# Second layer's queries and output gates of a Hawk/HGRN2 trunk: one Silu activation in place of a tanh and a VectorE product

## The chip, the cores and the metric

The kernel runs on one core of a Trainium2 chip. The time is the device time of one launch in microseconds, the median of several runs. The profiled execution is a further launch; its span runs from the first to the last instruction that the profiler records.

## What is computed

One inference step of a trunk of two layers with a model width of 1024, on 1024 prompt positions and on 8 sequences of 4 sample positions. Layer one is an RG-LRU block (convolution, gates, a linear recurrence, an output gate with SiLU). Layer two is an HGRN2 layer with eight heads of 128 keys and 128 values. The change lies in layer two, of which the reference says:

```python
def _hgrn_layer(x, g_norm, w_in, lb, o_gain, w_out, S0):
    xn = _rmsnorm(x, g_norm)
    u = (xn @ w_in).astype(jnp.float32)
    q, f, iv, gate = jnp.split(u, 4, axis=-1)
    q = jax.nn.silu(q).reshape(Bsz, T, H_B, DK_B)
...
    o, S_T = _hgrn2_chunked(q, k, v, log_g, S0)
    o = o * lax.rsqrt(jnp.mean(o * o, axis=-1, keepdims=True) + EPS) * o_gain.reshape(H_B, DV_B).astype(jnp.float32)
    y = (o.reshape(Bsz, T, INNER_B) * jax.nn.silu(gate)).astype(x.dtype)
    return x + y @ w_out, S_T.astype(x.dtype)
```

So silu(z) = z * sigmoid(z) is taken of the queries `q` and of the output gate `gate`. The forget gate `f` goes through a sigmoid. The keys, the decay and the values need no silu. The attention output `o` is linear in `q` and is normalized per head, so a constant factor on `q` cancels in the norm if the norm's epsilon is scaled with it.

## The kernel before

All activations lie transposed, features on the 128 partitions and the 1056 positions (1024 + 32) along the columns. Every product of weights and activations is made of three single-pass products of float32 values split into a high and a low part (`mm3`, L241 to L245: high times high, high times low, low times high), so TensorE does three matmuls for each product, and ScalarE, VectorE and GpSimd make the parts: ScalarE casts the high part (L380, L461, L1373, L1430), VectorE or GpSimd subtracts to get the low one (L325).

The order of the work is not written out by hand. Each operation is given to a planner, `Flow` (L52 to L199), with its engine, an estimated duration, the keys that it reads and writes, and a priority; the planner lays out a schedule and then emits the instructions of each engine in that order. Every engine runs its own instructions in order. There are two such plans. The first (L300 to L926) holds layer one and the first products of layer two; after it has found a schedule it also makes 3000 random trials (`search`, L167, with `SEARCH` at L24) that reshuffle operations of the first 60 estimated microseconds. These trials draw from the list of operations, so another list of operations gives another draw. The second plan (L929 to L1744) holds the rest, without random trials. Operations of TensorE marked `main` keep the order in which they are given.

Layer one ends with `out_last` (L650): for each of three column chunks of 352 it adds the output projection to the residual, sums squares for the norm (L432, L435), and scales and splits the normalized activations (`scaled_parts`, L458). L529 and L531 are evacuations of layer one's gates in its first chunk. Then come the first products of layer two, `first1` (L708): the queries of the first head (`i == 0`, L716 and L717) and its forget gate (`i == 1`, L720 to L722).

Layer two works head by head. For the first two heads, `item` (L996) evacuates each product of 352 columns: it takes the tanh of half the product on ScalarE (L1009) into a buffer `t`, one of a ring of five, and then, for the forget gate (`i == 1`), makes the decay row and the key row on GpSimd (L1012, L1014), and for the queries (`i == 0`) and the output gate (`i == 3`) computes (tanh(z/2) + 1) * z on VectorE (L1018). Since silu(z) is half of that, the row holds 2 silu(z). The values (`i == 2`) are only copied (L1004). Meanwhile `build` (L1349) makes sums and differences of activation blocks on VectorE (L1370), with casts on ScalarE and residues `t` on GpSimd. With them the six heads from the third on make each pair of projections with seven block products instead of eight (`seven`, L1403): results are added up on VectorE (`plus`, L1502) and each finished quarter of 264 columns goes to `settle` (L1505), which for queries and output gates takes the tanh (L1517) into the row itself and multiplies in place on VectorE (L1518).

What a head does besides its projections hangs in four `burst`s (L1332 to L1346), placed between the products of the projections: `own_gate` (L1063) scales the query row by the decay on VectorE (L1066), `levels01` to `levels3264` make the masked attention by levels of doubling block length (small matmuls at L1054, L1108, L1139, between rescalings of the rows by `scale`, L1036 to L1045), `states`, `advance` and `outs` carry the recurrent state, and `gated` (L1310) multiplies the normalized output by half the output gain, `hog`, and by the gate row (L1327). Two constants absorb the factor 2 of the rows: `hog` (L796), and `4 * EPS` in the norm (L1299).

A change of the function that ScalarE evaluates may need its table exchanged; the compiled program then holds a load of the table (ACT_TABLE_LOAD in the profile) ahead of the activation.

Of the kernel before, what the change touches and what calls it, by code (L numbers as in the profile page):

```python
# [19 lines left out]
ALU = mybir.AluOpType  # L20
# [191 lines left out]
def tile_trunk(ctx: ExitStack, tc: tile.TileContext, xT, prm, hc, w0, wg, wo0, w1, wo1, s_in,  # L212
# [22 lines left out]
    def pv(name):  # L235
        return P[:, PRM[name][0]:PRM[name][1]]
# [26 lines left out]
    def small(n):  # L263
        a = sm[:, smn[0]:smn[0] + n]
        smn[0] += n
        return a
# [31 lines left out]
    with ExitStack() as l0:  # L298
# [409 lines left out]
        def first1(i, c):  # L708

            if i not in ws1:  # L710
                ws1[i] = weights(w1[i], 1024)
            ps, pk = product(ws1[i], xcols(c), 1)
            q = chunk(c)
            if i == 0:
                o, ok = pairs[1][:, 0, q], [("R", 1, 0, c)]
                act(CH, lambda: S.activation(o, ps[:, :CH], AF.Tanh, scale=0.5), (pk,), ok, 0)  # L716
                dve(CH, lambda: V.scalar_tensor_tensor(o, o, 1.0, ps[:, :CH], op0=ALU.add, op1=ALU.mult), (pk, *ok), ok, 0)  # L717
            else:
                t, tk = next(ts)
                act(CH, lambda: S.activation(t, ps[:, :CH], AF.Tanh, scale=0.5), (pk,), (tk,), 0)  # L720
                for o, a, b, ks in ((ST, lc, lbc, [("ST", j, c) for j in range(3)]), (a_rows[0], lcn, lc, [("a", 0, c)])):
                    pool(CH, lambda o=o, a=a, b=b: G.tensor_scalar(o[:, q], t, a[:, :1], b[:, :1], op0=ALU.mult, op1=ALU.add),  # L722
                         (tk, ("sm1",)), ks, 0)
# [49 lines left out]
        def smalls1():  # L773
            def v(f, *a, **k):
                seq((("sm1",),), 6, ("DVE", lambda: f(*a, **k)))

            def ttv(o, a, b, op):
                v(V.tensor_tensor, o, a, b, op=op)

            nonlocal lc, lcn, lbc, hog  # L780
            mx, e0, e1, lb, lc, lcn, lbc, hog = (small(8) for _ in range(8))
            ttv(mx, pv("l0"), pv("l1"), ALU.max)
            ttv(e0, pv("l0"), mx, ALU.subtract)
            ttv(e1, pv("l1"), mx, ALU.subtract)
            seq((("sm1",),), 6, ("ACT", lambda: S.activation(e0, e0, AF.Exp)))
            seq((("sm1",),), 6, ("ACT", lambda: S.activation(e1, e1, AF.Exp)))
            ttv(mx, e0, e1, ALU.add)
            v(V.reciprocal, mx, mx)
            ttv(e0, e0, mx, ALU.mult)
            ttv(e1, e1, mx, ALU.mult)  # L790
            ttv(e1, e0, e1, ALU.add)
            ttv(lb, e1, e0, ALU.subtract)
            v(V.tensor_scalar, lc, lb, -0.5, 0.5, op0=ALU.mult, op1=ALU.add)
            v(V.tensor_scalar, lcn, lc, -1.0, None, op0=ALU.mult)
            ttv(lbc, lb, lc, ALU.add)
            v(V.tensor_scalar, hog, pv("og"), 0.5, None, op0=ALU.mult)  # L796

        def masks():

# [35 lines left out]
            v(V.tensor_scalar, bt, bf, 3.0, None, op0=ALU.is_le)  # L835
            ttv(bm, bm, bt, ALU.mult)

        hbr = hbi = hbd = cn = cp = lc = lcn = lbc = hog = None
# [90 lines left out]
    with ExitStack() as l1:  # L929
# [44 lines left out]
        def brow(h, i):  # L974
            return (Bs, eight("B")) if i else (B2, eight("B2"))
# [20 lines left out]
        def item(h, i):  # L996


            def evac(c, ps, pk):
                q = chunk(c)  # L1000
                ps = ps[:, :CH]
                if i == 2:
                    n = min(CH, SEQ - c * CH)
                    act(n, lambda: S.copy(VT[:, c * CH:c * CH + n], ps[:, :n]), (pk,), (("VT", c),), 0)  # L1004
                    if n < CH:
                        thrice(vrep, ps[:, n:], (pk,), "vrep")
                    return
                t, tk = next(ts)
                act(CH, lambda: S.activation(t, ps, AF.Tanh, scale=0.5), (pk,), (tk,), 0)  # L1009
                if i == 1:  # L1010
                    g, (b, bk) = Gs, brow(h, 1)
                    pool(CH, lambda: G.tensor_scalar(g[:, q], t, lc[:, h:h + 1], lbc[:, h:h + 1], op0=ALU.mult, op1=ALU.add),  # L1012
                         (tk,), GK, 0)
                    pool(CH, lambda: G.tensor_scalar(b[:, q], t, lcn[:, h:h + 1], lc[:, h:h + 1], op0=ALU.mult, op1=ALU.add),  # L1014
                         (tk,), bk, 0)
                else:
                    o, k = (SG[h], ykeys(h % 2, c * CH, CH)) if i else arow(h, 0)
                    dve(CH, lambda: V.scalar_tensor_tensor(o[:, q], t, 1.0, ps, op0=ALU.add, op1=ALU.mult), (pk, tk), k, 0)  # L1018

            return w1[4 * h + i], evac  # L1020

# [241 lines left out]
        def outs(h, s, sk):  # L1263
# [23 lines left out]
            for i in range(3):  # L1287
# [7 lines left out]
                else:  # L1295
                    pk = sk
                    act(128, lambda: S.activation(ons, o, AF.Square, accum_out=ssq[:32, 8:9]), (pk,), (("on", 2), ("ssq", 2)), 2)
                    r = slice(8, 9)
                dve(4, lambda r=r: V.tensor_scalar(rst[:, r], ssq[:, r], 1.0 / 128, 4 * EPS, op0=ALU.mult, op1=ALU.add),  # L1299
                    (("ssq", i),), (("rst", i),), 2)  # L1300
                fl.add("POOL", 0.85, lambda r=r: G.tensor_tensor(rst[:, r], rst[:, r], mhalf[:, r], op=ALU.pow),
                       (("rst", i),), (("rst", i),), 2)
# [7 lines left out]
        def gated(h, s, sk):  # L1310
            got = []
            for i in range(2):
                ps, pk = next(hg)

                def emit(i=i, ps=ps):
                    for n in range(4):
                        T.transpose(ps[:, n * 128:(n + 1) * 128], on[:, 4 * i + n, :], ident)

                pe(0.45, emit, (("kt", i),), (pk,))
                got.append((ps, pk, i * 512, 512))  # L1320
            o = s[:, 256:288]
            pe(0.17, lambda: T.transpose(o, ons, ident[:32, :32]), (("on", 2),), (sk,))
            got.append((o, sk, 1024, 32))
            yield
            for ps, pk, a, n in got:
                w = SG[h][:, a:a + n]
                dve(n, lambda ps=ps, w=w: V.scalar_tensor_tensor(w, ps, hog[:, h:h + 1], w, op0=ALU.mult, op1=ALU.mult),  # L1327
                    (pk,), ykeys(h % 2, a, n), 3)
            if h < H - 2:
                dma(yd[h], SG[h], ykeys(h % 2, 0, TOK), (("yd", h),), 4, 528)  # L1330
# [72 lines left out]
        def seven(h, a, b, order, at=()):  # L1403
# [4 lines left out]
            def ending(i, *args):  # L1408

                free = {0: 1, 1: 2}.get(i, 0)  # L1410
                postponed.append((free, lambda: settle(h, i, *args, args[2][0] == "s")))
                flush()

            def flush():
# [90 lines left out]
        def settle(h, i, a, c, ck, own):  # L1505

            q = slice(a, a + QT)
            if i == 1:
# [5 lines left out]
            else:  # L1514
                o, k = (SG[h], ykeys(h % 2, a, QT)) if i else arow(h, 0)
                k = k if i else k[a // QT::4]
                act(QT, lambda: S.activation(o[:, q], c, AF.Tanh, scale=0.5), (ck,), k, 0)  # L1517
                dve(QT, lambda: V.scalar_tensor_tensor(o[:, q], o[:, q], 1.0, c, op0=ALU.add, op1=ALU.mult), (ck, *k), k, 0, own)  # L1518


        dma(si.rearrange("p b v -> p (b v)"), s_in[0], (), two("si"), 4, 512)
# [293 lines left out]
```

## Time and profile before

| | |
|---|---|
| median of 3 runs | 1060.99 us (1060.94 to 1062.35) |
| span of the profiled execution | 1059.4 us |
| TensorE busy | 1050.1 us, 99% |
| VectorE busy | 842.2 us, 79% |
| ScalarE busy | 590.9 us, 56% |
| GpSimd busy | 540.0 us, 51% |
| table loads on ScalarE | 26, of 1283 ns each |

The median of the runs is 1.6 us above the span of the profiled execution. Lines such as L1018 are line numbers of the kernel before. In the profile PE is TensorE, DVE VectorE, ACT ScalarE, POOL GpSimd, and SP the engine that issues most transfers. Layer one's products fill the time up to about 500 us, the first two heads of layer two lie between about 490 and 595 us, the six others end at about 950 us, and the output projection and the last norm follow.

### The profile page before, as it was taken

How to read it: one execution, taken by the hardware profiler on the slowest of the kernel's cores; microseconds unless marked ns; L12 is line 12 of the kernel's file. 1: busy time of each engine (PE TensorE's matmuls, PEld its weight loads, DVE VectorE, ACT ScalarE, POOL GpSimd, SP SyncE). 2: the span in 40 equal slices, each digit the busy share in tenths (PEclk: the TensorE clock that was granted, in tenths of full speed). 3: DMA queues.
4: the chain of work that ended last, by engine and by line, in shares of the span. 5: the costliest groups of instructions: out<-in, count | busy, mean ns of one | idle time of the engine just before them, and what ended most of it. 6: DMA issues, size and time to landing. Idle time of an engine off the chain costs nothing.

```text
span 1059.4 us, 25677 instructions
## 1 busy us (share of the span) xinstructions
PE 1050.1 (99%) x9964; PEld 1021.2 (96%) x9964; DVE 842.2 (79%) x1671; ACT 590.9 (56%) x1339; POOL 540.0 (51%) x601
## 2 busy tenths in 40 slices
PE   9999999999999999999999999999999999999997
PEld 9999999999999999999999999999999999999986
DVE  7999996888888689265799988988979797994536
ACT  6568656877775875233354474646464555652324
POOL 3425343444544366555667555555545565551544
PEclk9999999999999999999999999999999999999998
DMA  8201112123842595340211121212121221355204
GB/s 297 68 27 45 54 51 74 57 60 100 255 145 63 177 294 162 127 136 28 71 44 38 45 101 44 92 45 92 35 91 54 72 70 66 117 177 167 84 3 164
DMA packets 70121, 103.07 MB, mean 97 GB/s; under 512 B 9200, under 2 KB 50160, under 8 KB 70000
## 3 DMA queue, kind: packets, MB, share of 16 engines
q1 hardware_dynamic: 67696, 98.67, 29.2%
q10 hardware_dynamic: 2304, 2.77, 0.8%
q8 instruction: 78, 1.28, 0.5%
q14 instruction: 43, 0.35, 0.1%
HBM read 71.05 MB, written 25.49 MB: 91 GB/s over the span
## 4 chain that ended last, share of the span: by engine, by line
PE 89%; DVE 6%; DMA 2%; POOL 1%; issue 1%; ACT 0%; ACTq 0%; POOLq 0%; DVEq 0%; SPq 0%
PE mm L243 24%; PE mm L244 24%; PE mm L245 24%; PE hg L569 1%; PE hg L1054 1%; PE hg L1163 1%; DVE R L1370 1%; PE hg L1273 1%; DMA wraw<-in_w_dram 1%; PE hg L1219 1%; PE hg L243 1%; PE hg L244 1%; PE hg L245 1%; PE hg L1275 1%; DVE tmp L1370 1%
## 5 line engine op out<-in xcount | busy, mean ns | idle before, releaser
L243 PE MATMUL mm<-xh,whi 128*128 128x352 f32 (+1 forms) x1143 | 358.6, 314 | 0.0
L245 PE MATMUL mm<-xh,wlo 128*128 128x352 f32 (+1 forms) x1143 | 353.2, 309 | 0.0
L244 PE MATMUL mm<-xl,whi 128*128 128x352 f32 (+1 forms) x1143 | 353.1, 309 | 0.0
L325 POOL TENSOR_TENSOR wlo<-wraw,whi 128x256 fp32r<-128x256 f32 (+3 forms) x184 | 203.3, 1122 | 178.6 <-ACT whi L380 81.2
L244 PEld LDWEIGHTS mm<-xl,whi 128*128 128x128 f32 x1143 | 215.1, 188 | 1.5
L243 PEld LDWEIGHTS mm<-xh,whi 128*128 128x128 f32 x1143 | 214.7, 188 | 1.5
L245 PEld LDWEIGHTS mm<-xh,wlo 128*128 128x128 f32 x1143 | 214.8, 188 | 0.0
L501 DVE SCALAR_TENSOR_TENSOR k<-xb,prm_sb,k 128x352 f32<-128x352 f32 (+2 forms) x144 | 90.1, 637 | 10.9 <-ACT k L498 7.7
L243 PE MATMUL mm<-t,whi 128*128 128x264 f32 (+1 forms) x306 | 89.3, 292 | 0.0
L244 PE MATMUL mm<-t,whi 128*128 128x264 f32 (+1 forms) x306 | 87.7, 287 | 0.0
L245 PE MATMUL mm<-t,wlo 128*128 128x264 f32 (+1 forms) x306 | 87.4, 286 | 0.0
L1503 DVE TENSOR_TENSOR k<-mm,k 128x264 f32<-128x264 f32 x144 | 60.2, 426 | 20.5 <-PE mm L245 17.4
L325 POOL TENSOR_TENSOR wlo<-R,whi 128x256 fp32r<-128x256 f32 x64 | 60.1, 959 | 24.7 <-ACT whi L1430 24.7
L584 POOL TENSOR_TENSOR k<-X 128x352 f32<-128x352 f32 x36 | 44.9, 1257 | 47.8 <-DVE R L585 38.6
L380 ACT CAST whi<-wraw 128x512 fp32r<-128x512 f32 (+2 forms) x83 | 46.1, 574 | 30.1 <-PE mm L244 16.1
L243 PEld LDWEIGHTS mm<-t,whi 128*128 128x128 f32 x306 | 57.6, 188 | 0.2
L245 PEld LDWEIGHTS mm<-t,wlo 128*128 128x128 f32 x306 | 57.7, 188 | 0.0
L244 PEld LDWEIGHTS mm<-t,whi 128*128 128x128 f32 x306 | 57.6, 188 | 0.0
L1430 ACT CAST whi<-wraw 128x512 fp32r<-128x512 f32 x52 | 32.1, 618 | 36.3 <-PE mm L245 16.8
L243 PE MATMUL mm<-yh,whi 128*128 128x352 f32 x153 | 49.9, 326 | 0.0
L245 PE MATMUL mm<-yh,wlo 128*128 128x352 f32 x153 | 49.4, 323 | 0.0
L244 PE MATMUL mm<-yl,whi 128*128 128x352 f32 x153 | 49.4, 323 | 0.0
(481 smaller groups left out, 2634.3 us busy)
## 6 DMA issues: line engine op xcount, KB each, us to landing
wraw<-in_w_dram SPq DMA_DIRECT2D x90, 256.0 KB, 2.7
wraw<-in_wo_dram SPq DMA_DIRECT2D x34, 192.0 KB, 2.5
si<-in_s_in_dram SPq DMA_DIRECT2D x8, 512.0 KB, 3.8
out_ss_out_dram<-si SPq DMA_DIRECT2D x8, 512.0 KB, 2.6
R<-in_w_dram SPq DMA_DIRECT2D x15, 256.0 KB, 2.5
sg<-x1b SPq DMA_DIRECT2D x21, 176.0 KB, 2.9
x<-sg SPq DMA_DIRECT2D x21, 176.0 KB, 1.8
R<-td SPq DMA_DIRECT2D x72, 44.0 KB, 2.0
```

What stands on the lines that cost most here:

```text
L243: T.matmul(out, wh, xh, start=first, stop=False)
L244: T.matmul(out, wh, xl, start=False, stop=False)
L245: T.matmul(out, wl, xh, start=False, stop=last)
L325: emit = lambda: e.tensor_tensor(b, x, a.bitcast(F32), op=ALU.subtract)
L380: act(m, lambda hi=hi, raw=raw, m=m: S.copy(hi[:, :m], raw[:, :m]), rk, (hk,), prio)
L501: dve(u, lambda src=src, dst=dst, sh=sh, k=k: V.scalar_tensor_tensor(dst, sh(src, k), pc("cw", 12 * k + m), dst, op0=ALU.mult, op1=ALU.add ...
L569: fl.add("PE", 0.62, lambda ps=ps, i=i, c=c: T.matmul(ps[:96, :CH], gs[:, i, :], ST[:96, chunk(c)], start=True, stop=True), (("gs",), *((" ...
L584: pool(CH, lambda x=x, a=a, b=b: G.tensor_tensor(x, a.bitcast(F32), b.bitcast(F32), op=ALU.add), (ak, bk), (xk,), 3)
L1054: T.matmul(ps[32 * j:32 * j + 32, n * w:n * w + w], B[:, o:o + 32], q(slice(o, o + 32)), start=True, stop=True, tile_position=(0, 32 * j))
L1370: dve(n, lambda: V.tensor_tensor(o, a, b, op=op), r, (w,), prio, True)
L1430: act(512, lambda: S.copy(hi, raw), (rk,), (hk,), 2)
L1503: dve(QT, lambda: V.tensor_tensor(o[0], z[0], u[0], op=ALU.add), (z[1], u[1]), (o[1],), 0)
```

## The change

Queries and output gates of layer two are made by one Silu activation on ScalarE, straight from the product (first two heads: from PSUM into the row; the others: from the quarter's sum into the row). The VectorE products of L717, L1018 and L1518 are gone, and the ring of `t` buffers is used by the forget gate alone. The rows now hold silu(z) instead of twice that, so the norm's epsilon is `EPS` instead of `4 * EPS`, and the gain is used as it is instead of halved; the small array `hog` and the instruction that makes it are gone. The forget gate keeps its tanh. No transfer is added or removed. Since the list of operations differs in both plans, both are planned anew.

```diff
@@ first1
             if i == 0:
                 o, ok = pairs[1][:, 0, q], [("R", 1, 0, c)]
-                act(CH, lambda: S.activation(o, ps[:, :CH], AF.Tanh, scale=0.5), (pk,), ok, 0)
-                dve(CH, lambda: V.scalar_tensor_tensor(o, o, 1.0, ps[:, :CH], op0=ALU.add, op1=ALU.mult), (pk, *ok), ok, 0)
+                act(CH, lambda: S.activation(o, ps[:, :CH], AF.Silu), (pk,), ok, 0)
@@ smalls1
-            mx, e0, e1, lb, lc, lcn, lbc, hog = (small(8) for _ in range(8))
+            mx, e0, e1, lb, lc, lcn, lbc = (small(8) for _ in range(7))
...
-            v(V.tensor_scalar, hog, pv("og"), 0.5, None, op0=ALU.mult)
@@ item, evac
-                t, tk = next(ts)
-                act(CH, lambda: S.activation(t, ps, AF.Tanh, scale=0.5), (pk,), (tk,), 0)
                 if i == 1:
+                    t, tk = next(ts)
+                    act(CH, lambda: S.activation(t, ps, AF.Tanh, scale=0.5), (pk,), (tk,), 0)
...
                 else:
                     o, k = (SG[h], ykeys(h % 2, c * CH, CH)) if i else arow(h, 0)
-                    dve(CH, lambda: V.scalar_tensor_tensor(o[:, q], t, 1.0, ps, op0=ALU.add, op1=ALU.mult), (pk, tk), k, 0)
+                    act(CH, lambda: S.activation(o[:, q], ps, AF.Silu), (pk,), k, 0)
@@ outs
-                dve(4, lambda r=r: V.tensor_scalar(rst[:, r], ssq[:, r], 1.0 / 128, 4 * EPS, op0=ALU.mult, op1=ALU.add),
+                dve(4, lambda r=r: V.tensor_scalar(rst[:, r], ssq[:, r], 1.0 / 128, EPS, op0=ALU.mult, op1=ALU.add),
@@ gated
-                dve(n, lambda ps=ps, w=w: V.scalar_tensor_tensor(w, ps, hog[:, h:h + 1], w, op0=ALU.mult, op1=ALU.mult),
+                dve(n, lambda ps=ps, w=w: V.scalar_tensor_tensor(w, ps, pc("og", h), w, op0=ALU.mult, op1=ALU.mult),
@@ settle
-                act(QT, lambda: S.activation(o[:, q], c, AF.Tanh, scale=0.5), (ck,), k, 0)
-                dve(QT, lambda: V.scalar_tensor_tensor(o[:, q], o[:, q], 1.0, c, op0=ALU.add, op1=ALU.mult), (ck, *k), k, 0, own)
+                act(QT, lambda: S.activation(o[:, q], c, AF.Silu), (ck,), k, 0)
```

More of the change, by code (lines that the diff above doesn't have):

```diff
@@ L778, in ttv @@
                 v(V.tensor_tensor, o, a, b, op=op)
-            nonlocal lc, lcn, lbc, hog
-            mx, e0, e1, lb, lc, lcn, lbc, hog = (small(8) for _ in range(8))
+            nonlocal lc, lcn, lbc
+            mx, e0, e1, lb, lc, lcn, lbc = (small(8) for _ in range(7))
             ttv(mx, pv("l0"), pv("l1"), ALU.max)
@@ L836, in masks @@
             ttv(bm, bm, bt, ALU.mult)
-        hbr = hbi = hbd = cn = cp = lc = lcn = lbc = hog = None
+        hbr = hbi = hbd = cn = cp = lc = lcn = lbc = None
         items = gate(0) + conv(0, True)
@@ L1410, in ending @@
                 free = {0: 1, 1: 2}.get(i, 0)
-                postponed.append((free, lambda: settle(h, i, *args, args[2][0] == "s")))
+                postponed.append((free, lambda: settle(h, i, *args)))
                 flush()
@@ L1503, in plus, with settle @@
             dve(QT, lambda: V.tensor_tensor(o[0], z[0], u[0], op=ALU.add), (z[1], u[1]), (o[1],), 0)
-        def settle(h, i, a, c, ck, own):
+        def settle(h, i, a, c, ck):
             q = slice(a, a + QT)
```

## The prediction

> **What bounds the kernel now.** I read the page's busy shares first, then the granted clock, then what TensorE waited for over the whole run, then busy time head by head, then the time lines at the places where TensorE did wait.
>
> ```profile
> span 1059.4 us, 25677 instructions
> PE 1050.1 (99%) x9964; PEld 1021.2 (96%) x9964; DVE 842.2 (79%) x1671; ACT 590.9 (56%) x1339; POOL 540.0 (51%) x601
> core 0: 1059.4 us, clock 0.996
> ```
>
> TensorE (PE) is busy 99% of the span at a granted clock of 0.996, so no clock is to be won. VectorE (DVE), from which the change takes work, is busy 79%. The most that its relief can give is what TensorE now loses by waiting for it. The whole-run list of TensorE's waits has five rows (us in total, times, longest):
>
> ```profile
> PE hg L730 <- DVE ones L255: 1.0, 1, 1.0
> PE hg L1108 <- DVE a L1036: 0.5, 1, 0.5
> PE mm L243 <- DVE sg L529: 0.5, 1, 0.5
> PE mm L1683 <- DVE sg L1673: 0.4, 1, 0.4
> PE hg L1054 <- DVE R L1066: 0.4, 1, 0.4
> ```
>
> Together 2.8 us of 1059.4. Only L1108 and L1054 lie at the second layer's beginning, where VectorE loses work; L730 and L529 belong to the start, L1683 to the last norm. Most of the removed instructions belong to the six heads from the third on (L1403 to L1518). Two windows of one head's length, two lengths apart:
>
> ```profile
> 688.40:745.10 56.70, 56.70 (x820) 54.82 (x813) 47.58 (x105) 30.66 (x80) 31.64 (x37) 1.00 0.20 68
> 801.80:858.50 56.70, 56.70 (x820) 54.82 (x813) 47.58 (x105) 30.66 (x80) 31.64 (x37) 1.00 0.20 69
> ```
>
> The columns are window, length, then busy us and count of PE, weight loads, DVE, ACT, POOL. TensorE is busy for the full 56.70 us with the same 820 instructions each time; VectorE has 9.1 us idle in each (56.70 - 47.6), ScalarE (ACT) 26. The heads repeat to the hundredth of a microsecond and none of the five waits lies in them: they are TensorE's alone.
>
> **The change part by part.** VectorE loses the products of L717, L1018 and L1518, and one operation of 8 columns at L796:
>
> ```profile
> L717 DVE SCALAR_TENSOR_TENSOR R<-R,mm x3: 521/521/522, 490.0 to 506.8; 128x352 f32<-128x352 f32 x3
> L1018 DVE SCALAR_TENSOR_TENSOR sg<-k,mm x6: 505/510/522, 517.2 to 592.6; 128x352 f32<-128x352 f32 x6
> L1018 DVE SCALAR_TENSOR_TENSOR R<-k,mm x3: 506/507/521, 542.0 to 551.6; 128x352 f32<-128x352 f32 x3
> L1518 DVE SCALAR_TENSOR_TENSOR sg<-sg,k 128x264 f32<-128x264 f32 x24 | 13.8, 595 | 0.0
> L1518 DVE SCALAR_TENSOR_TENSOR R<-R,k 128x264 f32<-128x264 f32 x24 | 13.4, 562 | 0.2 <-ACT R L1517 0.2
> ```
>
> That is 3 x 0.521 + 9 x 0.51 + 13.8 + 13.4 = 33.4 us of VectorE.
>
> *Heads three to eight: 0.* The 27.2 us of L1518 are 4.5 us a head; TensorE's full windows hide them, and VectorE's idle time only grows from 9.1 to about 13.6 us. The built program has TensorE's instructions in layer two in the same order as before, so nothing moves there.
>
> *L717: 0.* The step behind it waited for GpSimd (POOL), not for it:
>
> ```profile
> 506.82 0.52 DVE L717 SCALAR_TENSOR_TENSOR R<-R,mm 128x352 f32<-128x352 f32 x1 [3.20 <-ACT R L716]
> 511.09 1.27 DVE L1066 TENSOR_TENSOR R<-R,ST 128x1056 f32<-128x1056 f32 x1 [3.74 <-POOL ST L722]
> ```
>
> From 511.09 on VectorE has hardly a gap, so three L1018 at 517, 521 and 524 us push back what follows. The chain of work gives them 0.43 us each from start to start, and TensorE waits at 540:
>
> ```profile
> 517.28 0.43 DVE sg L1018
> 521.15 0.43 DVE sg L1018
> 524.46 0.43 DVE sg L1018
> ...
> 534.66 0.75 PE L1054 MATMUL hg<-R,sg 128*32 128x32 f32 x64
> 535.35 0.43 PE L243 MATMUL mm<-xh,whi 128*128 128x352 f32 x1
> ...
> 539.37 0.76 PE L1054 MATMUL hg<-R,sg 128*32 128x32 f32 x64
> 540.63 0.69 PE L1108 MATMUL hg<-R,a 128*16 128x16 f32 x64 [0.50 <-DVE a L1036]
> ```
>
> *First wait: -0.57.* The undisturbed group of 64 takes 535.35 - 534.66 = 0.69 us to the next instruction, the waiting one 540.63 - 539.37 = 1.26; the loss is 0.57. Without the three products VectorE reaches `a` of L1036 3 x 0.43 = 1.3 us sooner. In the order of the built program the same 30 sums of L1370 stand ahead of it as before, so that 1.3 us arrives whole. 1.3 is more than 0.57.
>
> *Second wait: -0.6, between 0 and -0.7.* The second head's start at 566 waits for L1066 and then for GpSimd's L1014 (0.3 us, in the view of L1054's waits):
>
> ```profile
> 562.46 0.47 ACT L1009 ACTIVATE k<-mm 128x352 f32<-128x352 f32 x1
> 563.57 0.97 DVE L1370 TENSOR_TENSOR tmp<-xh,tmp 128x264 f32<-128x264 f32 x1 [1.12 <-POOL t L325]
> 564.23 0.82 POOL L1012 TENSOR_SCALAR ST<-k,smalls 128x352 f32<-128x352 f32 x1
> 565.03 2.43 POOL L1014 TENSOR_SCALAR a<-k,smalls 128x352 f32<-128x352 f32 x1
> 565.25 1.24 DVE L1066 TENSOR_TENSOR R<-R,ST 128x1056 f32<-128x1056 f32 x1
> 566.55 1.44 PE L1054 MATMUL hg<-R,a 128*32 128x64 f32 x62 [0.36 <-DVE R L1066]
>   POOL a L1014: 0.3, 1
> ```
>
> The tanh is done at 562.93, but GpSimd takes it up at 564.23, behind residues (`t`, L325) whose inputs VectorE made late. Six L1018 less by then are 2.6 us; the built program puts one such residue in place of three between GpSimd's last two pairs but one, and two more L1370 (some 0.9 us) ahead of L1066. GpSimd can then start as much as 1.3 us sooner, and both waits, 0.4 + 0.3, mostly go. If GpSimd is late anyway, nothing goes. I take 0.6, near the rows.
>
> *ScalarE: 0, between 0 and +1.3.* Each tanh becomes one Silu on the same engine, 60 in all, with the same shapes. No Silu is in the trace; the nearest rows are the tanh itself and a plain copy:
>
> ```profile
> L1009 ACT ACTIVATE k<-mm 128x352 f32<-128x352 f32 x12 | 5.5, 461 | 4.4 <-PE mm L245 4.4
> L1004 ACT COPY sg<-mm 128x352 f32<-128x352 f32 (+1 forms) x6 | 2.6, 440 | 0.2 <-PE mm L245 0.2
> 83.01 1.28 ACT L588 ACT_TABLE_LOAD   x1
> 84.30 1.09 ACT L588 ACTIVATE R<-R 128x1056 f32<-128x1056 f32 x1
> 489.48 0.46 ACT L716 ACTIVATE R<-mm 128x352 f32<-128x352 f32 x1 [2.76 <-PE mm L245]
> ```
>
> 440 and 461 ns differ by 5%, so Silu gets tanh's duration. The built program has one table load more than before, 27 for 26, ahead of the first L716, and none between Silu and tanh after it. The load takes 1.28 us and its successor starts 0.01 us later; before L716 ScalarE was idle for 2.76 us, which hides it. Without that cover the eviction of one bank and what queues behind it (the next L716, then casts L461) would be 1.3 us late.
>
> *First layer: 0, between -1.0 and +3.* No removed operation but L796 runs there early, but the schedule is planned anew, and the first sixth of TensorE's order and much of VectorE's come out differently. VectorE is the tight engine there, and TensorE just waits for it as it enters the second third of the columns (next start 0.45 later instead of 0.16):
>
> ```profile
> 25.00:50.00 25.00, 24.42 (x152) 23.32 (x151) 24.41 (x55) 14.98 (x33) 9.77 (x11) 1.00 0.29 91
> 42.35 0.32 PE L243 MATMUL mm<-xh,X 128*128 128x352 f32 x1
> 42.80 0.44 PE L244 MATMUL mm<-xl,X 128*128 128x352 f32 x1
> L435 DVE TENSOR_TENSOR R<-R,xo x14: 509/522/1433, 20.4 to 46.8; 128x352 f32<-128x352 f32 x14
> ```
>
> In the new order two more sums of L435 and one product of L531 less stand ahead of that point: about one half-microsecond instruction late. Elsewhere a wait may go: L529's 0.5 and the 0.29 here are there to be lost. I take 0.
>
> Sum: -0.57 - 0.6 = -1.2 us. The profiled execution would go from a span of 1059.4 to 1058.2. The median of the runs, 1060.99, lies 1.6 us over that span; with the same 1.6 the forecast is **1059.8 us**. About 0.2%, 2.1 us, is what a measurement of this kernel can tell from no change: faster means below 1058.9, slower above 1063.1.
>
> **The rivals.**
>
> *Given back.* The wait at 540 goes, but GpSimd's L1014 (2.43 us while L1066 runs beside it, at 565) keeps the second, and the start loses half a microsecond: -0.57 + 0.5 = 0, **1060.9**. For it: GpSimd, not VectorE, ends the wait of 1.12 us at 563.57. Against: its inputs come from VectorE.
>
> *More waits go.* Besides the two, the new order loses L529's 0.5 us and the 0.29 at 42.8: -1.3 - 0.8 = -2.1, **1058.7**, and a little more if smaller stalls beside them go too. Against: nothing in the change aims there.
>
> *Slower, by the start.* In the first 60 us VectorE works without a gap (24.41 of 25 us), in order. Each instruction that the new order puts ahead of the second third's residues makes TensorE 0.43 to 0.5 us late once the slack is used up, and at 42.35 there is none. It turns the sign with the third such instruction (3 x 0.45 = 1.35 against -1.2) and is measurably slower with the eighth: +3.6 - 1.2 = +2.4, **1063.4**, and upwards. For it: VectorE's order there is changed in dozens of places. Against: I count about one.
>
> *Tables switched at each turn.* Were Silu's table without tanh, the order of the built program would switch 21 times, 21 x 1.28 = 27 us of ScalarE; its 26 us idle in each head hide most, a late eviction may cost 1 to 2 us: **1062**. Against: one load more in the program, and the trace of before has no more loads than the 26 of its program. The Trainium skill has the rule behind this rival: in "ScalarE activation tables: per-element evaluation and per-set limits", section "What a function is on this engine", functions of one set need no switch, and functions of two sets are one load of 1283 ns apart, which the 1.28 us above agrees with. The Trainium skill's page "ScalarE: Activation LUTs", section "What ACT_TABLE_LOAD costs", makes a switch about 2.66 us with a drain, so 21 of them an estimated 56 us by that page; the rows at 83.01 and 84.30 leave no room for a drain, and the measured 1.28 decides.
>
> *The change does what it sounds like.* 33.4 us less of VectorE end the run 33.4 us sooner: **1027.6**. Against: 99% and five waits.
>
> **How the numbers follow.** Forecast 0.44; given back 0.21; more waits go 0.19; slower by the start 0.13; tables 0.02; all of VectorE's time 0.01. Of these, "more waits go" lies about the bound and counts as faster: 0.19 + 0.01 = 0.20. Forecast, given back and tables are within 0.2%: 0.67, slightly less for tables: 0.66. Slower: 0.14. The range takes in all but the tails of both start cases and the last: 1057.4 (both waits, the start's -1.0 and a little more) to 1063.2 (no gain at 566, +3 at the start). The likeliest alone: 1058.9 to 1060.4.
>
> **What would show it.** Right: no tanh-then-product pair left; the windows of the heads still 56.70 us with VectorE near 43; the L1108 wait gone from TensorE's list and L1054's smaller; 27 table loads of 1.28 us; Silu near 461 ns for 352 columns. Wrong: heads shorter than 56.70 (then VectorE did hold TensorE there); a new wait of TensorE before 60 us; table loads after 510 us other than the last norm's; L1108 still waiting.

## The result, and the profile after

| | before | after |
|---|---|---|
| median of the runs, on one chip | 1061.13 us (1060.94 to 1062.35) | 1069.91 us (1069.4 to 1071.14) |
| span of the profiled execution | 1059.4 us | 1067.3 us |
| VectorE busy | 842.2 us | 816.2 us |
| table loads on ScalarE | 26 | 27 |

The changed kernel is slower: the ratio is 1.0084, with a 95% interval of 1.007 to 1.0098. The forecast was 1059.8 us, and 1069.9 us lies outside its range, on the other side of no change. Lines of the changed kernel are one to three lower than those of before (L1036 is L1034, L1054 is L1052, L1108 is L1106, L1370 is L1368, L1503 of some experiments is L1501).

The head of the page after, the line on its clock, and the five longest of the seven rows of what TensorE waited for (us in total, times, longest):

```profile
span 1067.3 us, 25614 instructions
PE 1054.5 (99%) x9964; PEld 1026.1 (96%) x9964; DVE 816.2 (76%) x1610; ACT 589.2 (55%) x1340; POOL 526.4 (49%) x601
core 0: 1067.3 us, clock 0.996
```

```profile
PE hg L1052 <- DVE sg L1034: 2.9, 1, 2.9
PE hg L729 <- DVE nr L442: 1.0, 1, 1.0
PE mm L1680 <- DVE sg L1670: 0.8, 1, 0.8
PE hg L1106 <- DVE a L1034: 0.5, 1, 0.5
PE mm L243 <- DVE k L1501: 0.5, 1, 0.5
```

VectorE's busy time fell by 26.0 us; the removed instructions had 33.4, so those that stay take 7.4 us longer. TensorE is still busy 99% of the span, with the same 9964 matmuls in 4.4 us more. So part of the loss is a new wait, 2.9 us at L1052, and part is not a wait at all: matmuls that are slower.

To see where, take the n-th matmul of one trace beside the n-th of the other; beyond the start both kernels issue them in the same order. The difference of their starts (after minus before) changes in five stretches. (The spans differ by 7.9 us; the profiled execution of after, 1069.42 us, is one of its two shortest.)

| stretch of before | difference at its end | gained or lost in it |
|---|---|---|
| start, to 63 us | +0.8 | -0.8 |
| layer one, to 518 us | +3.3 | -2.5 |
| beginning of layer two, to 561 us | +7.6 | -4.2 |
| second head's start, to 581 us | +7.0 | +0.5 |
| other heads, to 966 us | +8.2 | -1.2 |

**Layer one** is not late by waits. The same window of both kernels (busy us and count of PE, weight loads, DVE, ACT, POOL), first of before, then of after:

```profile
125.00:150.00 25.00, 25.00 (x159) 25.00 (x159) 23.54 (x45) 16.16 (x33) 10.55 (x15) 1.00 0.17 52
```

```profile
125.00:150.00 25.00, 25.00 (x157) 25.00 (x157) 24.06 (x51) 17.24 (x35) 11.59 (x15) 1.00 0.17 52
```

TensorE is full in both, at a granted clock of 1.00 in both, and gets through 157 matmuls where it got through 159. The mean distance between the starts of neighbouring 352-column matmuls is 159.3 ns before and 161.3 ns after in this window; in other windows the difference is as large or smaller, and over the 455 us it adds up to the 2.5 us above, with nothing to be seen in the list of waits.

**The beginning of layer two** holds the new wait. VectorE and GpSimd in the time line of after (start, length, engine, line, out<-in), just ahead of it:

```profile
514.31 1.27 DVE L1064 TENSOR_TENSOR R<-R,ST 128x1056 f32<-128x1056 f32 x1 [7.58 <-POOL ST L721]
...
538.88 0.42 DVE L1368 TENSOR_TENSOR R<-R,xh 128x264 f32<-128x264 f32 x1
539.34 2.85 DVE L1368 TENSOR_TENSOR R<-R,xl 128x264 f32<-128x264 f32 x2
...
543.91 1.22 DVE L1034 TENSOR_TENSOR R<-R,sg 128x512 f32<-128x512 f32 x1
545.05 0.68 DVE L1034 TENSOR_TENSOR sg<-sg 128x512 f32<-128x512 f32 x1
```

```profile
538.93 2.97 POOL L325 TENSOR_TENSOR wlo<-wraw,whi 128x512 fp32r<-128x512 f32 x2 [0.26 <-PE hg L1052]
541.86 2.73 POOL L325 TENSOR_TENSOR t<-R,t 128x264 fp32r<-128x264 f32 x3
```

The forecast rested on the 30 sums that stand between own_gate and the scalings of L1036. Their busy time in that stretch, first before (L1370, to 540.50), then after (L1368, to 546.95):

```profile
511.09:540.50 29.41, 14.61 (x30) 1.00 0.17 53
```

```profile
514.30:546.95 32.65, 18.71 (x30) 0.99 0.19 64
```

They are the same 30, and take 4.1 us longer. Half of that is in two sums of L1368: 0.42 us each when alone, they take 2.85 us together while two residues run on GpSimd beside them. The rest is spread over other sums, and L1034 at 543.91 adds another 0.5 us. In the kernel before those two residues ran only at 541.77, and at that place GpSimd was the one that waited, 3.99 us for two residues `t`, while VectorE went through L1036 at 0.67 us apiece:

```profile
537.83 3.99 POOL L325 TENSOR_TENSOR t<-R,t 128x264 fp32r<-128x264 f32 x2 [1.97 <-ACT t L1373]
541.77 3.19 POOL L325 TENSOR_TENSOR wlo<-wraw,whi 128x512 fp32r<-128x512 f32 x2
```

```profile
538.01 0.68 DVE L1036 TENSOR_TENSOR R<-R,sg 128x512 f32<-128x512 f32 x1
538.61 0.67 DVE L1036 TENSOR_TENSOR sg<-sg 128x512 f32<-128x512 f32 x1
```

TensorE pays in after, in its time line and in the windows (the column behind the five engines is the granted clock):

```profile
545.79 0.76 PE L1052 MATMUL hg<-R,sg 128*32 128x32 f32 x64 [2.88 <-DVE sg L1034]
547.09 0.73 PE L1106 MATMUL hg<-R,a 128*16 128x16 f32 x64 [0.53 <-DVE a L1034]
...
573.75 1.10 PE L1052 MATMUL hg<-R,a 128*32 128x64 f32 x64
```

```profile
543.00:546.60 3.60, 0.76 (x64) 0.65 (x64) 3.60 (x6) 1.85 (x4) 1.58 (x2) 0.99 0.19 68
546.60:550.00 3.40, 2.92 (x72) 2.91 (x73) 3.37 (x8) 1.39 (x3) 0.00 (x0) 0.50 0.02 5
```

Behind the wait the granted clock is halved for 3.4 us, and the matmuls of that stretch cost another 1.1 us. The last of the three rows above has no wait: the second head's start, which waited for L1066 in before, no longer does.

### The profile page after: what moved, and what is told of

It is laid out like the page before. It is cut to its first block, busy times and chain, and to the rows that moved or that the text cites. A ratio compares the mean times of both kernels' runs of the same rounds, so it can differ in the third digit from the quotient of the medians.

```text
span 1067.3 us, 25614 instructions
## 1 busy us (share of the span) xinstructions
PE 1054.5 (99%) x9964; PEld 1026.1 (96%) x9964; DVE 816.2 (76%) x1610; ACT 589.2 (55%) x1340; POOL 526.4 (49%) x601
## 4 chain that ended last, share of the span: by engine, by line
PE 90%; DVE 6%; issue 1%; DMA 1%; POOL 1%; ACT 0%; ACTq 0%; POOLq 0%; DVEq 0%
PE mm L243 25%; PE mm L244 24%; PE mm L245 24%; PE hg L1052 1%; PE hg L569 1%; PE hg L1271 1%; DVE R L1368 1%; PE hg L1217 1%; PE hg L1161 1%; PE hg L243 1%; PE hg L245 1%; PE hg L244 1%; PE hg L1273 1%; DMA wraw<-in_w_dram 1%; PE mm L1052 1%
## 5 line engine op out<-in xcount | busy, mean ns | idle before, releaser
L325 POOL TENSOR_TENSOR wlo<-wraw,whi 128x256 fp32r<-128x256 f32 (+3 forms) x184 | 199.2, 1100 | 189.7 <-ACT whi L380 104.5
L1501 DVE TENSOR_TENSOR k<-mm,k 128x264 f32<-128x264 f32 x144 | 60.4, 428 | 34.5 <-PE mm L245 32.7
L325 POOL TENSOR_TENSOR wlo<-R,whi 128x256 fp32r<-128x256 f32 x64 | 51.8, 830 | 25.4 <-ACT whi L1428 25.4
```

What stands on the lines that cost most here:

```text
L325: emit = lambda: e.tensor_tensor(b, x, a.bitcast(F32), op=ALU.subtract)
```

## The experiments

Two theories stand against each other. **The Silu costs** (on ScalarE, or through its table), or **the new order costs**: with another list of operations both plans come out differently, and what they place badly has nothing to do with Silu. If the order, the rivals within it are VectorE's own order, the neighbours on GpSimd, and where buffers come to lie.

**e1: Silu with the old order.** Each removed VectorE operation stays in its plan as an empty entry of its old duration, so the planner lays out every engine as in before; the entry emits nothing.

```diff
@@ first1, item, settle (from after)
+                dve(CH, lambda: None, (pk, *ok), ok, 0)
...
+                    dve(CH, lambda: None, (pk, tk), k, 0)
...
+                dve(QT, lambda: None, (ck, *k), k, 0, own)
```

> Both plans are given the operations of before, the three removed products as empty entries with their old duration, so that every engine keeps the order of before; Silu is used and the 61 instructions of VectorE are gone. Theory 'order': the new plans' order costs the time, not Silu; then this is 0.5 to 1.5 us faster than before (about 1060.0), with no wait of 2.9 us at L1052, and L1108's wait of 0.5 gone. Rival 'Silu': the function, its table load or the missing products cost the time in themselves; then it is about 1069, like the change.

Measured: 1060.18 us, ratio 0.9995 (0.9986 to 1.0003), span 1058.3 us. TensorE's waits no longer hold an L1108:

```profile
PE hg L730 <- DVE ones L255: 1.0, 1, 1.0
PE mm L1684 <- DVE sg L1674: 0.8, 1, 0.8
PE hg L1055 <- DVE R L1067: 0.5, 1, 0.5
PE mm L243 <- DVE sg L529: 0.3, 1, 0.3
```

The Silu itself costs nothing that can be measured; the 8.8 us belong to the new plans. But e1 also shows that the 1.3 us do not arrive whole. From the start of own_gate to the end of `a`, with the busy time of the 30 sums behind the length:

```profile
510.85:539.80 28.95, 14.91 (x30) 1.00 0.17 54
```

That is 0.45 us less than the 29.41 of before, though three products of 0.43 us are gone and VectorE's order is otherwise the same: the 30 sums take 0.3 us longer, and the eight scalings among them 8.25 us instead of 7.82. TensorE goes from the group of 64 to L1108 in 0.89 us (539.05 to 539.94) instead of 1.26, so 0.37 of the 0.57 us comes back. The second wait, at 565.78, is still there with 0.5 us.

**e3 and e4: one plan each.** e3 keeps the empty entries in the first plan only, e4 in the second plan only.

> Only the first plan (layer one and the first products of layer two) keeps the order of before by empty entries; the second plan is the change's. Theory 'order': 3.5 to 5 us slower than before (1064.5 to 1066), with the 2.9 us wait and the halved clock at about 543 us, and without the start's 0.8 us. Rival 'Silu': about 1069.

> Only the second plan keeps the order of before by empty entries; the first plan is the change's. Theory 'order': 0.8 us of the start stay, and the 2.5 us by which layer one fell behind stay if the first plan made them: 1061 to 1063.5; if they belong to the execution and not to the order, 1060 to 1061.5. No wait of 2.9 us. Rival 'Silu': about 1069.

Measured: e3 1066.96 us, ratio 1.0058 (1.0045 to 1.007); e4 1065.03 us, 1.0037 (1.0025 to 1.005). Each plan has its own loss, and each kernel is 1.0 to 1.5 us above the top of what was expected of it. Matched with before, e3 is even with it up to 518 us, 3.0 us late at 540, 3.5 at 581, and 5.6 behind a further wait at 647; e4 is 0.9 late at 63 us and 3.4 at 518, and loses nothing more. So the first plan's loss is the start and the pace, and the second plan's the wait at 540 and, in e3, one more, which was not expected. In e4 the trace, of the shortest of its five executions (1064.2 us), shows nothing beyond the start and the pace.

**e5: the new order without Silu.** At each Silu's place the old tanh and the old product are emitted; the planner knows of no VectorE time for the product.

```diff
@@ first1, item, settle (from after)
-                act(QT, lambda: S.activation(o[:, q], c, AF.Silu), (ck,), k, 0)
+                def both():
+                    S.activation(o[:, q], c, AF.Tanh, scale=0.5)
+                    V.scalar_tensor_tensor(o[:, q], o[:, q], 1.0, c, op0=ALU.add, op1=ALU.mult)
+                act(QT, both, (ck,), k, 0)
```

> The change's two plans, but each Silu is emitted as the tanh and VectorE product of before, at the place of the Silu, with hog and 4 * EPS as before: no Silu, no added table load, 61 more instructions of VectorE. Theory 'order': as slow as the change or a little slower, 1069 to 1073, with a wait of 2.9 us or more at 543 us. Rival 'Silu': about 1061.

Measured: 1077.62 us, ratio 1.0154 (1.014 to 1.0168). The wait at the beginning of layer two is there without any Silu (3.2 us at the line of L1054), and VectorE's unplanned products add 4.6 us of waits for L1503 in seven places. That the order costs is confirmed. The size, above the 1073 us expected, is only in part that of the products that no plan made room for: in the profiled execution (1079.84 us, the longest of five) the kernel is already 2.2 us late at 63 us, where after was 0.8 and none of the 60 products stands, and the granted clock is halved at 17.7, 546.7 and 656.0 us, where in after it was at 546.6 alone, the end of the run left aside.

**m1: the two residues moved away.** The base is e3, for its clean first layer. The two GpSimd residues `wlo` at 535.50 (e3's times), with the two loads that refill their buffers, go behind the residue `t` at 547.94. Nothing else moves.

```diff
@@ second plan, its last line (from e3)
-            fl.run()
+            fl.run(moves=(([197, 200, 217, 252], 45),))
```

> The kernel of e3_first_old (first plan with the old order, second plan as the change makes it; 1066.96 us) with one thing moved: the two GpSimd residues wlo of 128x512 at 535.50, and the two loads that refill their buffers, stand four GpSimd instructions later, behind the residue t at 547.94. Theory A (GpSimd holds VectorE up: the two L1370 that take 2.84 us together beside wlo instead of 0.87): VectorE reaches L1036 about 2 us sooner, the wait at L1054 falls from 3.1 to about 1.1 us, the stretch of half clock behind it (3.41 us long, so 1.7 us lost) goes too; time about 1063.3 us. Theory B (too many L1370 stand ahead of L1036, GpSimd does not matter): the wait stays at 3.1 us and the time at 1067.0 us.

The lines of this kernel and of m2 are seven higher than e3's. VectorE and GpSimd at the same place, then TensorE:

```profile
536.55 0.42 DVE L1377 TENSOR_TENSOR R<-R,xh 128x264 f32<-128x264 f32 x1
537.00 0.78 DVE L1377 TENSOR_TENSOR R<-R,xl 128x264 f32<-128x264 f32 x2
...
538.48 0.67 DVE L1043 TENSOR_TENSOR R<-R,sg 128x512 f32<-128x512 f32 x1
```

```profile
537.96 5.22 POOL L332 TENSOR_TENSOR t<-R,t 128x264 fp32r<-128x264 f32 x3 [1.63 <-ACT t L1380]
543.14 3.44 POOL L332 TENSOR_TENSOR wlo<-wraw,whi 128x512 fp32r<-128x512 f32 x2
```

```profile
540.24 0.76 PE L1061 MATMUL hg<-R,sg 128*32 128x32 f32 x64
541.11 0.69 PE L1115 MATMUL hg<-R,a 128*16 128x16 f32 x64
...
569.83 1.93 PE L1061 MATMUL hg<-R,a 128*32 128x64 f32 x64 [3.33 <-DVE R L1073]
```

The 30 sums, which take 18.70 us in e3, as in after, now take:

```profile
512.00:540.97 28.97, 15.62 (x30) 1.00 0.16 53
```

The two sums above take 0.78 us instead of 2.84, L1036 comes in time, and both waits and the half clock are gone: at 565 us the kernel is 3.8 us ahead of e3, although its start, in the same order, had come out 1.1 us later. Theory A holds, and more than the 2 us that I expected came back, because VectorE now has the run and GpSimd waits (`t` x3, 5.22 us instead of 2.73). But the time is 1068.93 us, ratio 1.0077 (1.0064 to 1.009), worse than e3: GpSimd, delayed, comes late to L1012 and L1014 of the second head, L1066 with it, and TensorE waits 3.3 us at 569.83 with a half clock of 6.8 us behind it, 6.1 us in all. That is the profiled execution, 1071.16 us, the longest of five; the shortest took 1067.24. The forecast of 1063.3 us failed by what the move set off further on.

**m2: one sum moved.** In e3, the further wait at 647 stands behind this (VectorE, GpSimd, TensorE):

```profile
642.98 3.28 DVE L1440 TENSOR_TENSOR R<-wraw,R 128x512 f32<-128x512 f32 x1
646.17 0.42 DVE L1503 TENSOR_TENSOR sg<-mm,k 128x264 f32<-128x264 f32 x1
646.52 0.42 DVE L1503 TENSOR_TENSOR k<-mm,k 128x264 f32<-128x264 f32 x1
```

```profile
643.60 3.24 POOL L325 TENSOR_TENSOR wlo<-wraw,whi 128x256 fp32r<-128x256 f32 x4
```

```profile
646.99 0.39 PE L243 MATMUL mm<-t,whi 128*128 128x264 f32 x1 [2.02 <-DVE k L1503]
```

L1440, 0.68 us when alone, lasts 3.28 us beside GpSimd instructions back to back (the end of an earlier one and the four residues, the last of which ends after it), and two L1503, which would free the bank that TensorE wants, are queued behind it. m2 puts L1440 behind these two.

```diff
@@ second plan, its last line (from e3)
-            fl.run()
+            fl.run(moves=(([624], 563),))
```

> The kernel of e3_first_old with one VectorE instruction moved: the L1440 that takes 3.28 us at 642.98 beside four GpSimd residues stands two instructions later, behind the two L1503 that were queued behind it. Theory A (it waits for the end of GpSimd's run, and the L1503 behind it with it, while an L1503, which reads PSUM, is not held up): L1440 stays long, the two L1503 come at 643, TensorE's wait of 2.0 us at 647 goes; 1064.9 us. Theory B (the L1503 wait for products or for GpSimd themselves): the wait stays, 1067.0 us.

```profile
643.25 0.42 DVE L1510 TENSOR_TENSOR sg<-mm,k 128x264 f32<-128x264 f32 x1
643.59 0.42 DVE L1510 TENSOR_TENSOR k<-mm,k 128x264 f32<-128x264 f32 x1
643.93 2.61 DVE L1447 TENSOR_TENSOR R<-wraw,R 128x512 f32<-128x512 f32 x1
```

As theory A has it: L1440 (here L1447) is still long, the two L1503 (here L1510) come first, and TensorE's 2.0 us at 647 are gone; matched with e3 the kernel gains 2.3 us there. 1.1 us of it go again at 656, where the same bank waits 0.85 us for another L1503. The time is 1066.48 us, 1.0053 (1.0041 to 1.0066): no difference from e3 that this measurement can tell, so the mechanism is shown by the rows, and the gain in the total is not.

**a1 and a2: the addresses.** The pace of layer one followed the first plan in every kernel so far: 159.3 ns with the old one (before, e1, e3), 161.3 ns with the new one (after, e4), to the end of the run, in stretches where all engines have the same order. In the built programs the 16 buffers of `xh` and `xl` and the 11 weight buffers lie at other SBUF addresses in the two groups: a buffer gets its place when it is first written, and the new start writes them in another order. a1 is after with one large tile cut by hand into before's places, every engine's order untouched; a2 is e1 with after's places.

```diff
@@ new_acts, and likewise the weight buffers (a1)
-            a = acts.tile([128, TOK], F32R, tag="P", name="xh")
-            b = acts.tile([128, TOK], F32R, tag="P", name="xl")
...
+        big = acts.tile([128, 16, TOK], F32R, tag="P", name="xp")
+        hs = [big[:, i] for i in [0, 15, 12, 9, 8, 5, 11, 4]]
+        ls = [big[:, i] for i in [14, 13, 10, 7, 6, 3, 1, 2]]
```

> The changed kernel, with the order of every engine untouched, but with the 16 buffers of xh and xl and the 11 weight buffers (wraw, whi, wlo) at the SBUF addresses that they have in the kernel before; in the changed kernel the same buffers lie at other addresses, because the start's new order takes them in another sequence. Theory A (the addresses set the pace of the 352-column matmuls): in 125 to 150 us the mean from start to start goes from 161.3 to 159.3 ns, and about 2.5 us of layer one come back: 1067.4 us. Theory B (the order of the start or of the other engines sets it): 161.3 ns and 1069.9 us as before.

> The kernel of e1_both_old (one Silu, every order as in the kernel before; 1060.18 us) with the same buffers of xh, xl, wraw, whi and wlo at the addresses that they have in the changed kernel. Theory A (addresses): 161.3 ns from start to start in 125 to 150 us instead of 159.3, and 1062.7 us. Theory B: 159.3 ns and 1060.2 us.

One row each of the windows of a1, of e1 and of a2 (the count in brackets behind PE's busy time is the one to look at: 157 was the slow pace; for a1 the next window is shown, where after had 157 and before 159 too; from 125 us it has 158):

```profile
150.00:175.00 25.00, 25.00 (x159) 25.00 (x158) 20.93 (x34) 13.41 (x34) 12.30 (x18) 1.00 0.23 69
```

```profile
125.00:150.00 25.00, 25.00 (x159) 25.00 (x158) 22.91 (x44) 16.15 (x32) 11.62 (x15) 1.00 0.18 52
```

```profile
125.00:150.00 25.00, 25.00 (x157) 25.00 (x156) 22.91 (x44) 16.36 (x32) 11.74 (x15) 1.00 0.18 52
```

Theory A holds in both directions. a2 runs at 161.4 ns and takes 1063.57 us, 1.0026 (1.0016 to 1.0035), against e1's 0.9995: 3 us for nothing but addresses. a1 runs at 160.2 ns in the window that was forecast, half way, and at 159.2 in the next, and has won 2.3 of the 2.5 us over after by 522 us. Its time, 1068.83 us, 1.0073 (1.0059 to 1.0086), is 1.4 us above the forecast and shows only part of that. In the profiled execution 1.3 us go at 550, where the half clock lasts 6.8 us instead of 3.4, and 3.4 us at 650, where after lost 0.3 us behind L1438 and a1 waits 2.0 us behind the same sum, as e3 does, with a half clock that e3 hasn't. That execution, 1071.13 us, is the longest of five; the others took 1068.07 to 1068.97 at a higher clock, and no trace shows what they lost there.

**a3: activations alone.** As a1, but the weight buffers stay where after has them; one run.

> The changed kernel with only the 16 buffers of xh and xl at the addresses of the kernel before; the weight buffers stay where the changed kernel has them. If the pace of the 352-column matmuls hangs on the activations' addresses, the mean from start to start in 125 to 150 us comes back to 159.3 ns; if on the weight buffers' addresses, it stays at 161.3 ns; if on both together, it lies between or elsewhere.

Measured: 160.2 ns from 125 us and 159.2 ns in the next window, the same as a1 to the hundredth, 1069.11 us in one run. The addresses of `xh` and `xl` decide the pace; moving the weights' as well adds nothing.

**a4 and a5: other layouts.** a4 is e1 with all buffers in ascending order, a5 e1 with each `xl` two buffers below its `xh`.

```diff
@@ new_acts (from a2), a5
+        hs = [big[:, i] for i in [15, 11, 10, 3, 2, 14, 7, 6]]
+        ls = [big[:, i] for i in [13, 9, 8, 1, 0, 12, 5, 4]]
```

> The kernel of e1_both_old with the 16 buffers of xh and xl and the 11 weight buffers laid out in plain ascending order, a third layout. If addresses set the pace, the mean from start to start in 125 to 150 us may come out at neither 159.3 nor 161.3 ns, and the time moves with it by about 1.25 us for each nanosecond: 1060 us at 159.3, 1062.7 us at 161.3, and below 1060 us if the pace is better than either. If only something else that goes with the two layouts matters, it stays at 159.3 ns and 1060.2 us.

> The kernel of e1_both_old with a fourth layout of xh and xl: each xl two buffers (8448 bytes) below its xh, as it is in five of eight pairs of the kernel before and in none of the three layouts that ran at 161.3 ns; the order of the pairs is a new one, and the weight buffers lie as in the kernel before. Theory A (what counts is how far apart the two parts lie that TensorE reads one behind the other): in the four layouts seen, the step from xh to an xl two below took 160.8 ns and the step back 159.1 ns, so that the pace in 125 to 150 us comes near 159.5 ns and the time near 1060.5 us. Theory B (the distance does not matter, each layout has a pace of its own): most likely 161 ns or more, as three of four layouts had, and 1063 to 1064 us.

The window of a4, then of a5:

```profile
125.00:150.00 25.00, 25.00 (x157) 25.00 (x156) 22.76 (x44) 16.24 (x33) 11.16 (x15) 1.00 0.16 52
```

```profile
125.00:150.00 25.00, 25.00 (x159) 25.00 (x158) 22.88 (x44) 16.15 (x32) 11.60 (x15) 1.00 0.17 52
```

a4: 161.3 ns, 1064.05 us, 1.003 (1.0019 to 1.0041), the slow pace again. a5: 159.5 ns, 1060.9 us, 1.0 (0.999 to 1.0009), as forecast from the distance of the two parts. One layout made to a rule and found right speaks for the distance, but the premise was miscounted, and the traces speak against distance alone. By the lists of places six of the eight pairs of before lie two buffers apart, not five, and two of after's do. In a4 all eight pairs have the same distance, one buffer; yet over 56 groups of 24 matmuls between 63 and 480 us the mean step from `xh` to `xl` is 160.7 to 162.4 ns in every second pair and 162.6 to 164.1 in the others. In a5, also with one distance, the mean steps back go from 157.8 to 162.3 ns. So the place of the buffers counts beside their distance, and why stays open.

**s1: another draw.** The changed kernel with another seed for the first plan's random trials.

```diff
@@ Flow.search
-        rng = Random(1)
+        rng = Random(2)
```

> The changed kernel with another seed for the first plan's random trials; the list of operations, the second plan and all work are the same. If the loss of the first 500 us is the draw's and not the Silu's, the start (0.8 us late against before at 63 us) and the pace (161.3 ns) come out differently, while the second layer's losses, whose order does not hang on the seed, stay at 3 to 6 us; the time then lies anywhere from 1064 to 1071 us. If the Silu itself cost something in layer one, both stay as they were, 1069.9 us.

Measured: 1073.14 us, ratio 1.0116 (1.0101 to 1.0131). The start is 2.7 us late at 63 us where after was 0.8, the pace is slow here too (161.2 ns), and the second layer's losses stay: 2.8 us of wait at L1052 and 2.0 us behind L1501. The time is above the bracket that I gave: the start loses 1.9 us more than after's, and the wait at 650 with a half clock behind it 3.3 us more, in the profiled execution. That the pace would come out differently did not hold, so s1 alone does not separate the draw from Silu. It is a1 and a2 that show the pace to be the addresses'. Of the three draws seen, that of the kernel before is the best.

No version ran measurably faster than before. The best is e1, at 1060.18 us beside 1060.7 us.

## Why the prediction was wrong, point by point

- **The failed step is "First wait: -0.57".** It said that the 1.3 us "arrives whole" because the same 30 sums stand ahead of L1036. Even in e1, where every order is kept, only 0.45 us of it arrives and 0.37 of the 0.57 us comes back. In after, 32.65 us pass from the start of own_gate to the end of `a` where it was 29.41, though VectorE has three products less to do: 1.3 us less of products, 4.1 us more for the same 30 sums, 0.5 us more for a scaling. The count of instructions ahead was right; their durations were not those of before, since GpSimd's instructions lie elsewhere beside them. m1 shows it: with two GpSimd instructions moved away the 30 sums go from 18.70 to 15.62 us and the wait is gone. I had counted VectorE's order and not looked at what each sum has beside it on GpSimd. The term came out at -0.57 forecast, +3.0 for the waits and +1.1 for the half clock behind them.
- **"First layer: 0, between -1.0 and +3"** failed in size and in cause: +3.3. Of it 2.5 us are the pace, by the addresses of `xh` and `xl`, a term that the sum did not have. The other 0.8 are the start's. At the place that the working named, 42.35 us, one matmul came 0.45 us behind the one before it; at the same place of after it is 0.73, so 0.28 us more. Where the rest is lost no run separates. After, e4, a1 and a3, with the new first plan, are 0.8 to 0.9 us late at 63 us; of the eight traces with the old one seven lie between -0.2 and +0.3 us, but m1 is 0.9 us late as well, so a single execution can differ as much.
- **"Second wait: -0.6"** held in the number: -0.5, and the row at 573.75 shows no wait. GpSimd takes the tanh up 0.10 us after its end (570.45 us) where it took 1.30 in before, as the working had it. But "six L1018 less" is not the reason: in e1 they are gone too, GpSimd takes 1.31 us, and a wait of 0.5 us stays. Whether it is the residues' new place or the 4.2 us by which TensorE, and so the tanh, comes later in after is not separated.
- **"Heads three to eight: 0"** held in all but two places: the 0.3 us at 650 behind L1438 (L1440 in e3), and 0.7 us at about 930 for L1501. The first is 2.0 or 2.1 us in e3, e5, m1, a1, a3 and s1, the other kernels with the new second plan except m2: L1438 takes 1.91 us in after and 3.27 to 3.29 in those six, so the profiled execution of after had luck there. In the rest the difference stays the same to the tenth. A window of one head's length in after, with VectorE at 43.95 us as forecast ("near 43"):

```profile
695.70:752.40 56.70, 56.70 (x817) 54.81 (x810) 43.95 (x97) 30.16 (x80) 29.77 (x38) 1.00 0.21 68
```

- **"ScalarE: 0"** and the tables held. Silu takes tanh's time (461 ns were taken), there is one load more, and none between Silu and tanh:

```profile
L1515 ACT ACTIVATE sg<-k 128x264 f32<-128x264 f32 x24 | 10.0, 422 | 13.2 <-DVE k L1501 13.0
...
L1016 ACT ACTIVATE sg<-mm 128x352 f32<-128x352 f32 x6 | 2.8, 462 | 4.8 <-PE mm L245 4.8
...
L716 ACT ACT_TABLE_LOAD x1 | 1.3, 1283 | 0.0
```

- **The rival "slower, by the start"** had the sign, at 0.13, but not the mechanism: it asked for eight VectorE instructions ahead in the first 60 us, and the start gave less than a tenth of the loss. No rival had a new wait at 540. Two of the signs that would show the prediction wrong are there: "L1108 still waiting", at 0.5, and "a new wait of TensorE before 60 us", 0.3 us at 42.30.
- As a forecast of the edit alone the number came out, in part by luck: for the span it said 1058.2 us, and e1, the edit without the new order, has 1058.3. But of e1's 1.1 us only about 0.4 are the first wait's; 0.24 are won before 63 us and 0.2 at about 930, which the sum did not have, and the second wait gives nothing. The medians differ by 0.5 us, which the interval does not tell from no change.
- Two sums do not follow from their own terms. "More waits go" gives 1060.99 - 2.1 = 1058.9, not 1058.7; the ends of the range give 1058.7 (-0.57 - 0.7 - 1.0) and 1063.4 (-0.57 + 3.0) where 1057.4 and 1063.2 stand. The result lies above all of them.

## What to carry to other kernels

Where a planner lays out the order, an edit that frees time is also a new draw of the plan, and a kernel in which TensorE is busy 99% can lose more by the draw than the edit can give. Judge the two apart: leave empty entries of the old duration in the plan, and see what the edit does on its own. When the order of an engine is compared, compare also which instructions of VectorE and GpSimd come to lie beside each other, and compare the addresses of the buffers.

## What the runs showed of the hardware

- **VectorE and GpSimd hold each other up, for one instruction or for several.** In after, two sums beside two residues end 0.29 us behind the end of one residue each (540.75 behind 540.46, 542.19 behind 541.90): each waited for one. L1440 in e3 stood 2.6 us (3.28 less 0.68): it ended 0.55 us behind the third of four residues (646.25 behind 645.70) and before the fourth (646.83). The same sum took 1.91 us in after. At 537.83 in before it was GpSimd that needed 3.99 us for two residues while VectorE ran without a gap. An L1503, with one operand in PSUM, keeps its 0.42 us within GpSimd's run (646.17 and 646.52 in e3, where the run ends at 646.84). The Trainium skill, "SBUF — State Buffer", section "SBUF: two separate sides", calls the port that the two share an exclusive lock, which whoever starts first has "for the whole instruction". The two sums in after agree with that; in the other two places the one that came second waited through several instructions of the other, not one.
- **The pace of matmuls hangs on where the moving operand lies**: 159.2 to 161.4 ns from start to start for 352 columns, at a granted clock of 1.00 and with no wait in the profile, over four layouts of `xh` and `xl`. No row names it; only the count in a window shows it.
- **The granted clock is halved for 3.4 us, or twice that, behind a wait of about 3 us** (2.8 to 3.3), in each kernel that had one (0.50 in the window from 546.6 to 550.0). Behind waits of 2.0 or 2.1 us it was halved in m1, a1, s1 and e5 and not in e3 and a3. The Trainium skill, "TensorE: Matmul & The Clock Gate", section "What's actually happening", gives such a window as 3413 ns, free-running, and halves the clock after an idle one of that length; the length agrees, the idle time here, 2.9 us, was shorter.
